# VectorE in GpSimd's place for four sums of the gate's weights

## The chip, the cores and the metric

One program on one core of a Trainium2 chip. The metric is the device time of one execution in microseconds (us). The engines are TensorE (PE: matmuls; PEld: its weight loads), VectorE (DVE), ScalarE (ACT), GpSimd (POOL) and SyncE (SP). GpSimd and SyncE here also issue the loads and stores.

## What is computed

One layer of a decoder trunk, 512 tokens, width 1024, float32: an RMS norm, one wide projection, a block-sparse attention branch and a gated recurrence branch, their merge, an output projection that is added to the residual, and last a gated embedding. The change lies in the last two lines:

```python
h = h + merged.astype(dt) @ w_out[i]
ple = (p[i] @ w_ple[i]).astype(f32) * jax.nn.sigmoid((h @ w_ple_gate[i]).astype(f32))
h = h + ple.astype(dt)
```

`h` is 512 x 1024 and `w_ple_gate` 1024 x 1024.

## The kernel before

Each float32 product is done as three matmuls of a reduced type. An operand is split in a high part (ScalarE copies it, rounding; names ending in `h`) and a low part (VectorE subtracts the high part from the operand; names ending in `l`), and high x high, low x high and high x low are summed. So every weight that arrives has to pass ScalarE and then VectorE before TensorE can use it.

The last stage, `h @ w_ple_gate`, is a 2 x 2 block product in seven half-size products instead of eight (Strassen's scheme in Winograd's form). `product(i, tt)` is one of two token tiles of product i: 12 matmuls of 128 x 512, four steps of the inner dimension k with three matmuls each. They run in the order 1, 5, 6, 7, 4, 3, 2, with the small products `pe` (the embedding, 6 matmuls a tile) between them. Results lie in the PSUM banks `ga`, `gb` and `gc`: products 6, 7 and 4 add up in the two `gb` banks, so before product 7 writes a bank, VectorE must have read it (`keepr = gb + keep`, L1348), and likewise `keepb` before product 4.

The operands of the seven products are sums and differences of blocks. Those of the tokens (`b..`, `bl`, `bt`, `bu`) come from `pairs_of_h`, out of the eight blocks `hf` of the residual (L1262); `b2l` of the fourth pair is the low part that product 1 needs for its last k step. Those of the weights come from `weights_of_g`, a generator that the code advances step by step: `a11`, `a22`, `a21` are blocks of the weight as loaded, of two tiles each, 128 x 1024. It makes

- `s1 = a21 + a22` for product 5 (L1143, tiles named `gs`), and in place `a11 = a11 - a21` for product 7 (L1145, tiles named `wf`): two instructions each, on GpSimd;
- `s1 = a22 - a11` for product 6 (L1152) and `s1 = a12 - s1` for product 3 (L1164), on VectorE;
- the high and low parts `w1h`, `w1l` to `w7h`, `w7l` in `halves_of`, on ScalarE and VectorE.

The weights of the stage are loaded by eight transfers of 512 KB on GpSimd's queue (L276), each as soon as its tile is free. Two of them stand between GpSimd's own sums, and the last two take the tiles of `a21`, which the differences L1145 read last.

The embedding's weights `w_p` (L1229 on SyncE's queue) pass one after the other through two slots of `pb`. A slot is filled again once VectorE has read it (`pwl`, L1231). ScalarE runs in order: behind the high parts `pwh` of these weights stand the high parts `w3h` and the sigmoids of the first output tiles. The two banks `pe` of the first embedding are free for the second when VectorE has multiplied them into the outputs (L1302).

TensorE's order is written out by hand. The order on the other engines is set by a list scheduler, from the dependencies, from priorities (`tc.high_priority`) and from edges that give an order only (`behind(inst, other)`); it decides from its own estimates, so a change to one instruction can move others.

## Time and profile before

| | |
|---|---|
| median of 3 runs | 449.94 us (449.64 to 450.37) |
| profiled execution | 449.9 us |
| its span, first to last instruction | 448.1 us |
| TensorE busy | 441.2 us, 98% |
| VectorE busy | 341.6 us, 76% |
| ScalarE busy | 287.5 us, 64% |
| GpSimd busy | 88.1 us, 20% |
| mean granted TensorE clock | 0.994 |

The profiled execution's time is 1.8 us above its span: what lies before the first and after the last instruction. A row of the timeline gives start, duration, engine, line, operation, output<-inputs, sizes, and in brackets how long the engine had been idle and what ended it. A row of VectorE or ScalarE covers the instruction's whole length, and the next one can begin a little before its end; the distance of two starts is what an instruction costs its engine when nothing holds it. Matmuls are pipelined: they show 0.39 us each and start every 0.227 us.

### The profile page before, as it was taken

The page shows a single profiled execution, that of the slowest core. Times are in us where ns is not written, and L with a number is a line of the kernel's source. Part 1 is how long each engine was busy: PE and PEld are TensorE (multiplying, and loading weights), DVE is VectorE, ACT ScalarE, POOL GpSimd, SP SyncE. Part 2 cuts the span into 40 slices and gives each one's busy share as a digit, 9 for nine tenths or more (in the row PEclk, how much of TensorE's full clock was granted, in tenths as well). Part 3 has the DMA queues.
Part 4 walks back from the last instruction along what each step waited for, and adds up shares of the span by engine and source line. Part 5 has one row for each costly group of instructions (what it writes and reads, how often), then busy time and mean ns, then how long its engine had stood idle before and what let it go on. Part 6 is the DMA issues. An engine that isn't in the chain of part 4 may idle for free.

```text
span 448.1 us, 7514 instructions
## 1 busy us (share of the span) xinstructions
PE 441.2 (98%) x2646; PEld 366.3 (82%) x2646; DVE 341.6 (76%) x662; ACT 287.5 (64%) x541; POOL 88.1 (20%) x147
## 2 busy tenths in 40 slices
PE   9999999999999999999999999999999999979996
PEld 8888888888888888888888888878888888868886
DVE  5869496777899797949888575565479779999852
ACT  5858584637779888967988697873234444355611
POOL 1000100000000432041403141501220103520242
PEclk9999999999999999999999999999999999989999
DMA  8803333357595463273423745455540666623222
GB/s 251 337 1 94 116 119 118 106 198 180 157 200 133 150 169 124 84 188 120 141 95 88 229 142 153 120 177 137 155 133 26 204 201 189 206 68 94 94 95 94
DMA packets 36709, 63.69 MB, mean 142 GB/s; under 512 B 7616, under 2 KB 19776, under 8 KB 36672
## 3 DMA queue, kind: packets, MB, share of 16 engines
q0 software_dynamic: 10848, 34.87, 25.2%
q1 hardware_dynamic: 25536, 28.27, 22.6%
q8 instruction: 21, 0.34, 0.3%
q14 instruction: 16, 0.13, 0.1%
q10 hardware_dynamic: 288, 0.07, 0.1%
HBM read 50.87 MB, written 7.08 MB: 129 GB/s over the span
## 4 chain that ended last, share of the span: by engine, by line
PE 95%; DVE 3%; issue 1%; ACT 0%; DVEq 0%
PE gb L305 10%; PE ga L305 10%; PE h L305 7%; PE bq L305 5%; PE ub L305 5%; PE bg L305 5%; PE ak L435 5%; PE ag L305 5%; PE bf L305 5%; PE ua L305 5%; PE aq L435 5%; PE av L435 5%; PE bi L435 5%; PE gb L1289 4%; PE gc L1289 2%; PE pe L1220 2%
## 5 line engine op out<-in xcount | busy, mean ns | idle before, releaser
L287 DVE TENSOR_TENSOR wl<-wf,wh 128x1024 fp32r<-128x1024 f32 (+1 forms) x70 | 76.6, 1095 | 32.9 <-ACT wh L286 31.5
L286 ACT ACTIVATE wh<-wf 128x1024 fp32r<-128x1024 f32 (+1 forms) x70 | 67.0, 957 | 49.3 <-PE ub L305 12.0
L276 POOL DMA_DIRECT2D wf<-in_w_tr_dram x30 | 16.2, 540 | 110.0 <-DVE wl L287 74.4
L924 POOL DMA_DIRECT2D pb<-pb x56 | 27.7, 501 | 36.5 <-DVE pb L913 16.1
L305 PE MATMUL ga<-xh,wh 128*128 128x512 f32 x64 | 25.2, 394 | 0.0
L305 PE MATMUL gb<-xh,wh 128*128 128x512 f32 x64 | 25.1, 393 | 0.0
L305 PE MATMUL ga<-xh,wl 128*128 128x512 f32 x64 | 24.9, 389 | 0.0
L305 PE MATMUL gb<-xl,wh 128*128 128x512 f32 x64 | 24.9, 389 | 0.0
L305 PE MATMUL ga<-xl,wh 128*128 128x512 f32 x64 | 24.9, 389 | 0.0
L305 PE MATMUL h<-mh,wh 128*128 128x512 f32 x64 | 24.9, 389 | 0.0
L305 PE MATMUL h<-ml,wh 128*128 128x512 f32 x64 | 24.9, 389 | 0.0
L305 PE MATMUL h<-mh,wl 128*128 128x512 f32 x64 | 24.9, 389 | 0.0
L305 PE MATMUL gb<-xh,wl 128*128 128x512 f32 x64 | 24.9, 389 | 0.0
L908 ACT ACTIVATE pb<-pb,ps 128x128 f32<-128x128 f32 (+3 forms) x32 | 17.6, 551 | 7.6 <-DVE ps L906 7.6
L276 POOL DMA_DIRECT2D wf<-in_w_tok_dram x8 | 4.4, 552 | 76.8 <-ACT avv L495 45.2
L1305 POOL TENSOR_TENSOR out<-out,pb 128x512 f32<-128x512 f32 (+1 forms) x8 | 10.3, 1300 | 38.9 <-DVE out L1302 38.8
L276 POOL DMA_DIRECT2D wf<-in_w_up_dram x16 | 8.7, 541 | 41.7 <-DVE wl L287 23.4
L910 ACT ACTIVATE pb<-pb,ps 128x128 f32<-128x128 f32 (+3 forms) x32 | 15.8, 550 | 0.1
L305 PEld LDWEIGHTS ga<-xh,wh 128*128 128x128 f32 x64 | 12.0, 188 | 2.8 <-issue 0.4
L305 PEld LDWEIGHTS gb<-xh,wh 128*128 128x128 f32 x64 | 12.0, 188 | 2.7 <-issue 0.2
L305 PEld LDWEIGHTS ga<-xh,wl 128*128 128x128 f32 x64 | 12.0, 188 | 2.6
L305 PEld LDWEIGHTS gb<-xh,wl 128*128 128x128 f32 x64 | 12.0, 188 | 2.5
(575 smaller groups left out, 1383.2 us busy)
## 6 DMA issues: line engine op xcount, KB each, us to landing
wf<-in_w_tr_dram POOLq DMA_DIRECT2D x30, 512.0 KB, 4.0
wf<-in_w_tok_dram POOLq DMA_DIRECT2D x8, 512.0 KB, 3.6
wf<-in_w_g_dram POOLq DMA_DIRECT2D x8, 512.0 KB, 4.2
wf<-in_w_up_dram POOLq DMA_DIRECT2D x16, 256.0 KB, 3.0
wf<-in_w_o_dram POOLq DMA_DIRECT2D x8, 512.0 KB, 4.4
wf<-in_w_tok_dram SPq DMA_DIRECT2D x6, 512.0 KB, 6.9
bias<-in_ed_dram SPq DMA_DIRECT2D x8, 256.0 KB, 5.1
xres<-in_xT_dram SPq DMA_DIRECT2D x8, 256.0 KB, 3.0
```

The lines of the kernel that those rows point to most:

```text
L276: (G if len(wraw) >= FAR else nc.sync).dma_start(raw, ap)
L286: rounds[i] = A.activation(hi, wraw[i], AF.Copy)
L287: low = V.tensor_tensor(lo, wraw[i], hi.bitcast(F32), op=OP.subtract)
L305: dense.append(PE.matmul(ps, a[:, k, :], b[k], start=(n == 0), stop=(n == tot - 1)))
L435: dense.append(PE.matmul(banks[t], a[:, s_], b[:, kk, :], start=(k == 0 and i == 0), stop=(k == KD - 1 and i == 2)))
L908: A.activation(p_, p_, AF.Exp, bias=st[:, 0:1], scale=-1.0, accum_out=st[:, 1:2])
L910: A.activation(p_, p_, AF.Copy, scale=st[:, 2:3])
L924: (G if both and b % 2 else nc.sync).dma_start(pt[32 * b:32 * b + 32, a], z[32 * a:32 * a + 32, b])
L1220: dense.append(PE.matmul(bk[:, c], a[:, ts_], b[:, c], start=(n == 0), stop=(n == 5)))
L1289: dense.append(PE.matmul(dst[i][tt][:, c], a[:, 128 * tt:128 * tt + 128], b[:, c], start=(k == 0 and m == 0 and i in (1, 6, 5)), stop=(k = ...
L1305: (adder or G).tensor_tensor(o3, o3, h_, op=OP.add)
```

## The change

The four instructions L1143 and L1145 go from GpSimd to VectorE. The low parts of product 7's third and fourth k step, made by the form of `halves_of` with its own tiles (`apart`), are written ahead of the other two in the code and get an edge that puts them behind the last low part made by the other form, which is product 6's (`w6l`).

```diff
             for k in range(2):
-                split(hs[k], ls[k], src[:, k])
+                A.activation(hs[k], src[:, k], AF.Copy)
+                low = V.tensor_tensor(ls[k], src[:, k], hs[k].bitcast(F32), op=OP.subtract)
+                if i == 7:
+                    behind(low, lows[-1])
             return list(zip(hs, ls))
...
-        V.tensor_tensor(l_, src, h_.bitcast(F32), op=OP.subtract)
+        lows.append(V.tensor_tensor(l_, src, h_.bitcast(F32), op=OP.subtract))
...
         for k in range(2):
-            G.tensor_tensor(s1[k], a21[k], a22[k], op=OP.add)
+            V.tensor_tensor(s1[k], a21[k], a22[k], op=OP.add)
         for k in range(2):
-            G.tensor_tensor(a11[k], a11[k], a21[k], op=OP.subtract)
+            V.tensor_tensor(a11[k], a11[k], a21[k], op=OP.subtract)
...
+        second = halves_of(7, 2, a11[1], "w7", "YB")
         halves_of(7, 0, a11[0], "w7")
-        wt[7].extend(halves_of(7, 2, a11[1], "w7", "YB"))
+        wt[7].extend(second)
```

Below, the order on VectorE at three places; TensorE's order is the same in both kernels. Line numbers behind the change are 1 to 4 higher (L1131 becomes L1134, L1143 L1146, L1145 L1148, L1152 L1155, L234 of these splits L1125). `pb` is scratch space of the token sums, `hf_4085` the last block but one of the residual, `w5l`, `w1l` low parts of the weights of products 5 and 1.

First, before product 1. Before:

```order
L1204 TENSOR_TENSOR pb<-hf_4034,pb 128x256
L234 TENSOR_TENSOR bl2l<-hf_4034,bl2h 128x512
L234 TENSOR_TENSOR bt2l<-pb,bt2h 128x512
L1210 TENSOR_TENSOR bu2l<-pb,bu2h 128x512
L234 TENSOR_TENSOR w5l_4117<-gs_4110,w5h_4115 128x512
L1262 TENSOR_TENSOR hf_4085<-h_4060,xres_4054 128x512
L1131 TENSOR_TENSOR w1l_4057<-wf_3942,w1h_4056 128x1024
L234 TENSOR_TENSOR w5l_4118<-gs_4110,w5h_4116 128x512
L1193 TENSOR_TENSOR pb<-hf_4085 128x256
L234 TENSOR_TENSOR b2l<-hf_4085,b2h 128x256
```

The same stretch on VectorE after the change:

```order
L1208 TENSOR_TENSOR pb<-hf_4034,pb 128x256
L1146 TENSOR_TENSOR gs_4110<-wf_4105,wf_3997 128x1024
L234 TENSOR_TENSOR bl2l<-hf_4034,bl2h 128x512
L234 TENSOR_TENSOR bt2l<-pb,bt2h 128x512
L1148 TENSOR_TENSOR wf_3881<-wf_3881,wf_4052 128x1024
L1214 TENSOR_TENSOR bu2l<-pb,bu2h 128x512
L1266 TENSOR_TENSOR hf_4085<-h_4060,xres_4054 128x512
L1125 TENSOR_TENSOR w5l_4117<-gs_4110,w5h_4115 128x512
L1134 TENSOR_TENSOR w1l_4057<-wf_3942,w1h_4056 128x1024
L1125 TENSOR_TENSOR w5l_4118<-gs_4110,w5h_4116 128x512
L1197 TENSOR_TENSOR pb<-hf_4085 128x256
L234 TENSOR_TENSOR b2l<-hf_4085,b2h 128x256
```

The second sum and the first difference now stand ahead of `b2l`. The first sum stands further up, between the previous `b2l` and `hf_4034`; the second difference stands right behind this `b2l`.

Second, the low parts for products 6 and 7 on VectorE. Before:

```order
L234 TENSOR_TENSOR bt3l<-pb,bt3h 128x256
L234 TENSOR_TENSOR w7l_4241<-wf_3942,w7h_4239 128x512
L1131 TENSOR_TENSOR w6l_4204<-gs_4109,w6h_4203 128x1024
L1131 TENSOR_TENSOR w6l_4208<-gs_4110,w6h_4207 128x1024
L1164 TENSOR_TENSOR gs_4109<-wf_4247,gs_4109 128x1024
```

The same stretch after the change:

```order
L234 TENSOR_TENSOR bt3l<-pb,bt3h 128x256
L1134 TENSOR_TENSOR w6l_4204<-gs_4109,w6h_4203 128x1024
L1134 TENSOR_TENSOR w6l_4208<-gs_4110,w6h_4207 128x1024
L1125 TENSOR_TENSOR w7l_4237<-wf_3942,w7h_4235 128x512
L1168 TENSOR_TENSOR gs_4109<-wf_4247,gs_4109 128x1024
```

The low part of product 7 went from ahead of the two `w6l` to behind them.

Third, on VectorE from the first `keepr` on. Before:

```order
L1348 TENSOR_TENSOR keepr_4167<-gb_4161,keep_4165 128x512
L1231 TENSOR_TENSOR pwl_4257<-pb,pwh_4256 128x512
L1131 TENSOR_TENSOR w4l_4288<-wf_3995,w4h_4287 128x1024
L1348 TENSOR_TENSOR keepr_4168<-gb_4162,keep_4166 128x512
L1131 TENSOR_TENSOR w4l_4292<-wf_3997,w4h_4291 128x1024
L1241 STREAM_TRANSPOSE restart<-hf_4148 128x4x4x32
```

The same stretch after the change:

```order
L1352 TENSOR_TENSOR keepr_4167<-gb_4161,keep_4165 128x512
L1134 TENSOR_TENSOR w4l_4288<-wf_3995,w4h_4287 128x1024
L1352 TENSOR_TENSOR keepr_4168<-gb_4162,keep_4166 128x512
L1134 TENSOR_TENSOR w4l_4292<-wf_3997,w4h_4291 128x1024
L1235 TENSOR_TENSOR pwl_4257<-pb,pwh_4256 128x512
L1245 STREAM_TRANSPOSE restart<-hf_4148 128x4x4x32
```

`pwl_4257`, which frees a slot of `pb` for the last of the embedding's weights, went behind three others. On ScalarE `pwh_4256` went behind the two `w4h` in the same way. On GpSimd only its loads are left in this stretch, in the same order.

## The prediction

> **What bounds the kernel now.** I read the head of the page and its chain first, then TensorE's waits, then the timelines of the engines around the one long wait.

> ```profile
> span 448.1 us, 7514 instructions
> PE 441.2 (98%) x2646; PEld 366.3 (82%) x2646; DVE 341.6 (76%) x662; ACT 287.5 (64%) x541; POOL 88.1 (20%) x147
> ...
> PE 95%; DVE 3%; issue 1%; ACT 0%; DVEq 0%
> ```

> TensorE is the bound: 98% of the span and 95% of the chain that ended last. Only what shortens TensorE's own row of work counts, so the next view is its waits.

> ```profile
> PE ga L1289 <- DVE b2l L234: 2.5, 1, 2.5
> ```

> There is one in all the kernel (beside the start): 2.5 us in product 1, for the low part `b2l`. TensorE's timeline there, and at two later points that I need:

> ```profile
> 392.76 0.39 PE L1289 MATMUL ga<-w1h,b2h 128*128 128x512 f32 x1
> 395.63 0.79 PE L1289 MATMUL ga<-w1h,b2l 128*128 128x512 f32 x1 [2.49 <-DVE b2l L234]
> ...
> 398.76 0.40 PE L1289 MATMUL ga<-w1l,b0h 128*128 128x512 f32 x1
> 399.00 0.39 PE L1289 MATMUL ga<-w1h,b2h 128*128 128x512 f32 x1
> ...
> 411.24 0.39 PE L1289 MATMUL gb<-w7h,bu0h 128*128 128x512 f32 x1
> ...
> 424.84 0.39 PE L1220 MATMUL pe<-pwh,ph 128*128 128x512 f32 x1
> ```

> From the first matmul of product 7 (411.24) to that of the second `pe` (424.84) stand 60 matmuls: 13.60 / 60 = 0.227 us each. So the matmul at 395.63 could have begun at 392.99: the stall cost 2.64 us. The eight matmuls from 395.63 to 399.00 took 3.37 us where 1.81 is normal: 1.56 more. The stretches show why (PEclk, the third figure from the right, is the granted clock):

> ```profile
> 395.63:399.00 3.37, 3.37 (x9) 2.67 (x9) 3.27 (x5) 2.09 (x4) 0.21 (x1) 0.54 0.49 156
> 399.00:411.24 12.24, 12.24 (x56) 10.13 (x54) 12.24 (x18) 7.59 (x13) 0.00 (x0) 1.00 0.17 45
> ```

> After the stall the clock was 0.54. Stall and slow spell make 4.20 us, the most that this place can give back. The second row also shows VectorE busy for all of 12.24 us: it is the next bound.

> Why `b2l` was late is seen in VectorE's timeline beside GpSimd's:

> ```profile
> 377.43 2.14 DVE L234 TENSOR_TENSOR b2l<-hf,b2h 128x256 fp32r<-128x256 f32 x1
> 380.04 0.69 DVE L1262 TENSOR_TENSOR hf<-h,xres 128x512 f32<-128x512 f32 x1 [0.47 <-PE h L305]
> ...
> 383.51 2.89 DVE L234 TENSOR_TENSOR bl2l<-hf,bl2h 128x512 fp32r<-128x512 f32 x1
> 386.32 2.89 DVE L234 TENSOR_TENSOR bt2l<-pb,bt2h 128x512 fp32r<-128x512 f32 x1
> 389.14 0.68 DVE L1210 TENSOR_TENSOR bu2l<-pb,bu2h 128x512 fp32r<-128x512 f32 x1
> 389.74 0.68 DVE L234 TENSOR_TENSOR w5l<-gs,w5h 128x512 fp32r<-128x512 f32 x1
> ...
> 392.68 2.57 DVE L1193 TENSOR_TENSOR pb<-hf 128x256 f32<-128x256 f32 x1
> 395.17 0.41 DVE L234 TENSOR_TENSOR b2l<-hf,b2h 128x256 fp32r<-128x256 f32 x1
> 395.73 0.42 DVE L234 TENSOR_TENSOR bt3l<-pb,bt3h 128x256 fp32r<-128x256 f32 x1
> 396.07 1.22 DVE L1152 TENSOR_TENSOR gs<-wf,wf 128x1024 f32<-128x1024 f32 x1
> 397.21 0.68 DVE L1262 TENSOR_TENSOR hf<-h,xres 128x512 f32<-128x512 f32 x1
> ```

> ```profile
> 376.89 2.40 POOL L1143 TENSOR_TENSOR gs<-wf,wf 128x1024 f32<-128x1024 f32 x1 [4.28 <-DMA wf<-in_w_g_dram]
> 379.24 0.57 POOL L276 DMA_DIRECT2D wf<-in_w_g_dram  x1
> 383.20 2.65 POOL L1143 TENSOR_TENSOR gs<-wf,wf 128x1024 f32<-128x1024 f32 x1 [3.40 <-DMA wf<-in_w_g_dram]
> 385.82 2.85 POOL L1145 TENSOR_TENSOR wf<-wf,wf 128x1024 f32<-128x1024 f32 x1
> ...
> 392.24 2.73 POOL L1145 TENSOR_TENSOR wf<-wf,wf 128x1024 f32<-128x1024 f32 x1 [2.71 <-DVE w1l L1131]
> ```

> Four VectorE rows are long, and each began inside one of GpSimd's four sums and ended 0.28 to 0.55 us after it (379.57 after 379.29; 386.40 after 385.85; 389.21 after 388.67; 395.25 after 394.97): they waited for it and then did their own work. The other rows of the same sizes take 0.42 and 0.68.

> **The change part by part.** *Removed from VectorE:* the waits. By starts, a 128x512 costs 0.60 (389.14 to 389.74), a 128x256 0.34 (395.73 to 396.07). `bl2l` and `bt2l` took 2.81 and 2.82, the `pb` row 2.49: 2.21 + 2.22 + 2.15 = 6.58 us won behind 380.04. The 1.80 of the row at 377.43 lies ahead of an `hf` that waited for TensorE anyway.

> *Added to VectorE:* four instructions of the kind at 396.07, same operation and size, 1.14 by starts. The first sum comes behind the row at 377.43, which then ends by 377.85, and is done before 379.1: `hf` still starts at 380.04, cost 0. The second sum and the first difference stand ahead of `b2l`, 2.28; the second difference behind it, 1.14.

> *Product 1.* `b2l` starts at 395.17 - 6.58 + 2.28 = 390.87 and ends by 391.3; TensorE wants it at 392.99. 1.7 us to spare, so stall and slow spell go: -4.20 for TensorE here.

> *Product 7.* TensorE now asks for it at 411.24 - 4.20 = 407.04, and it needs `keepr` read first:

> ```profile
> 404.51 1.05 ACT L1128 ACTIVATE w7h<-wf 128x1024 fp32r<-128x1024 f32 x1
> ...
> 410.15 0.68 DVE L1348 TENSOR_TENSOR keepr<-gb,keep 128x512 f32<-128x512 f32 x1
> 410.75 0.68 DVE L1231 TENSOR_TENSOR pwl<-pb,pwh 128x512 fp32r<-128x512 f32 x1
> ...
> 416.38 1.23 DVE L1131 TENSOR_TENSOR w3l<-gs,w3h 128x1024 fp32r<-128x1024 f32 x1 [0.89 <-ACT w3h L1128]
> ...
> 421.73 0.68 DVE L1302 TENSOR_TENSOR out<-out,pe 128x512 f32<-128x512 f32 x1
> ```

> VectorE has the same instructions ahead of `keepr` plus three: 410.15 - 6.58 + 3.42 = 406.99. One wait appears: with `w7l` behind the `w6l`, only two 128x256 rows lie between the subtraction L1155 and the `w6l` that needs ScalarE's copy of its result. The copy takes 1.05 (row at 404.51), so `w6l` can start 1.22 + 1.05 and two hand-overs of 0.05 (`b2l` ended at 395.58, TensorE began at 395.63) after the subtraction's start, 2.37, while VectorE is free after 1.14 + 0.34 + 0.34 = 1.82: 0.55 idle. That is the price of the new edge. A gap of 0.22 before (395.17 + 0.34 to 395.73) goes. So `keepr` starts at about 407.3, ends at 408.0, and TensorE stalls 1.0 us: of 4.20, 3.2 is left. What is late next is thus VectorE itself.

> *The second `pe`.* TensorE would ask for its bank 60 matmuls on, at 408.0 + 13.60 = 421.6. The bank comes free by the row at 421.73, which hangs on this chain: `pwl` at 410.75 frees the slot, the last `w_p` lands, ScalarE copies it, then `w3h`, then VectorE's `w3l` (idle 0.89 before it):

> ```profile
> 414.37 0.63 ACT L1230 ACTIVATE pwh<-pb 128x512 fp32r<-128x512 f32 x1 [0.79 <-DMA pb<-in_w_p_dram]
> 415.29 1.06 ACT L1128 ACTIVATE w3h<-gs 128x1024 fp32r<-128x1024 f32 x1 [0.29 <-PE gb L1289]
> ```

> This `pwl` now stands behind `w4l`, `keepr`, `w4l`: 407.3 + 0.60 + 1.14 + 0.60 + 1.14 = 410.8, no earlier than before. So `pwh` stays at 414.4; `w3h` no longer waits for TensorE and follows at 414.9, 0.4 earlier; the row at 421.73 moves to 421.3, ends at 422.0. TensorE stalls 0.4 and starts the second `pe` at 422.05 instead of 424.84: 2.8 us won.

> *The rest:* from there TensorE runs as before, with VectorE half idle.

> ```profile
> 424.84:443.88 19.04, 19.04 (x100) 16.47 (x98) 8.45 (x12) 3.96 (x7) 7.53 (x6) 1.00 0.29 101
> ```

> *GpSimd's queue:* the load at 379.24 no longer waits behind a sum; the last two wait for differences that end earlier than GpSimd's. Their cover is the 10 us until their first use; cost 0, gain 0.

> The sum against the profiled execution: 449.9 - 2.8 = 447.1, and its 449.9 is the median's 449.94.

> [...]

> **The rivals.**

> *Both new stalls fail to come:* `keepr` and the bank are in time, all 4.20 is kept: 445.7. For it: 1.0 and 0.4 are differences of long sums. Against: VectorE had no gap there, and before had only 0.4 in hand (`keepr` ended at 410.83, product 7 began at 411.24).

> *The 1.0 us stall drops the clock too:* 1.56 lost in product 7; the `pe` stall of 0.4 goes with it, so 447.1 + 1.1 = 448.2. No row shows a stall of that length; it is nearer to none than to 2.64.

> *A sum waits for its load on VectorE:* the first sum's load landed at 376.89 where it is wanted at 377.8, with 1.1 more before `hf` is late. It would have to land 4.8 us later to use up the 2.8: 449.9.

> *The long rows have another cause* and stay, transfers say: this ends slower. Then `keepr` starts 3.42 + 0.55 later, at 414.1, product 7 at 414.85 instead of 411.24: 453.5. It decides once less than 3.6 of the 6.58 goes. Against it: the stretch 360 to 370 has more DMA than 380 to 390 (0.70 against 0.60, second figure from the right) and no sum on GpSimd, and a row like `bl2l` took 0.68 there:

> ```profile
> 360.00:370.00 10.00, 10.00 (x46) 8.29 (x45) 7.62 (x13) 3.64 (x6) 1.06 (x2) 1.00 0.70 201
> 380.00:390.00 10.00, 10.00 (x45) 8.29 (x45) 9.93 (x10) 4.69 (x7) 6.04 (x3) 1.00 0.60 184
> ```

> ```profile
> 362.35 0.68 DVE L234 TENSOR_TENSOR bl0l<-hf,bl0h 128x512 fp32r<-128x512 f32 x1
> ```

> [...]

> **How the numbers follow.** Forecast 0.60 (446.6 to 447.6: a few tenths on each hand-over); full gain 0.13; clock drop 0.15; late load 0.06; long rows stay 0.06. About 0.2% (0.9 us) is what a measurement can tell from none. The first three are faster, 0.88; the late load is the same, 0.06; the last slower, 0.06. From the full gain, 445.6, to the clock drop with 0.4 for the hand-overs, 448.6, lie 0.88 of the chance.

> **What would show it.** Right: no VectorE row over 1.3 us between 376 and 396; no wait for `b2l`; PEclk 1.00 from 395 to 399; two TensorE waits, about 1.0 for `keepr` ahead of product 7 and 0.4 for `out` ahead of the second `pe`; 0.5 idle before `w6l`. Wrong: long rows that stay, a clock under 1.00 behind product 7's start, or a VectorE wait for a load of `w_g`.

## The result and the profile after

The changed kernel takes 447.25 us (median of 6 runs, 447.08 to 448.36) against 450.02 of the kernel before: a ratio of 0.9942, interval 0.9929 to 0.9955. Forecast were 447.1 and 445.6 to 448.6. The profiled execution took 447.09, its span 445.3, 2.8 us less than before. The page's head and chain, and TensorE's waits:

```profile
span 445.3 us, 7514 instructions
PE 439.7 (99%) x2646; PEld 364.1 (82%) x2646; DVE 338.1 (76%) x666; ACT 287.8 (65%) x541; POOL 76.3 (17%) x143
...
PE 97%; DMA 1%; ACT 0%; SPq 0%; DVE 0%; issue 0%; DVEq 0%
```

```profile
PE gb L1293 <- ACT w4h L1131: 0.9, 1, 0.9
```

The wait for `b2l` is gone. VectorE has left the chain (3% to 0%), and its busy time fell by 3.5 us although it does four instructions more: what it lost was waiting that the profile had counted as work. A wait of 0.9 us ahead of product 7 is new. (A further 0.3 in the attention branch stands in this profile and not in the second one of the same kernel; product 1 is no later for it, as its matmul at 392.71 stood at 392.76 before.) TensorE's timeline at the three places:

```profile
392.71 0.39 PE L1293 MATMUL ga<-w1h,b2h 128*128 128x512 f32 x1
392.94 0.39 PE L1293 MATMUL ga<-w1h,b2l 128*128 128x512 f32 x1
...
406.77 0.39 PE L1293 MATMUL gb<-w6l,bt3h 128*128 128x512 f32 x1
408.09 0.47 PE L1293 MATMUL gb<-w7h,bu0h 128*128 128x512 f32 x1 [0.94 <-ACT w4h L1131]
408.40 0.39 PE L1293 MATMUL gb<-w7h,bu0l 128*128 128x512 f32 x1
...
421.55 0.39 PE L1293 MATMUL gb<-w4l,bu3h 128*128 128x512 f32 x1
421.88 0.50 PE L1224 MATMUL pe<-pwh,ph 128*128 128x512 f32 x1
422.21 0.40 PE L1224 MATMUL pe<-pwh,pl 128*128 128x512 f32 x1
```

At `b2l` the matmuls follow each other every 0.23 us. Product 7 could have begun 0.227 after 406.77, at 407.00, and began at 408.09: 1.09 lost, and 0.08 more because the first matmul behind the stall took 0.31 (408.09 to 408.40) instead of 0.227. The second `pe` lost 0.10 and again 0.10 in its first matmul. Of the 4.20 that the place could give back, 1.37 went again: 2.83 is left, which is what the span shows. The clock stayed up in all of it (third figure from the right):

```profile
395.00:399.00 4.00, 4.00 (x19) 3.34 (x18) 3.65 (x7) 2.35 (x4) 0.00 (x0) 1.00 0.31 100
...
407.00:412.00 5.00, 4.07 (x18) 3.30 (x18) 5.00 (x8) 2.18 (x3) 0.00 (x0) 1.00 0.17 56
```

VectorE's rows that answer to those of before:

```profile
377.38 0.38 DVE L234 TENSOR_TENSOR b2l<-hf,b2h 128x256 fp32r<-128x256 f32 x1
377.69 1.22 DVE L1146 TENSOR_TENSOR gs<-wf,wf 128x1024 f32<-128x1024 f32 x1
379.99 0.69 DVE L1266 TENSOR_TENSOR hf<-h,xres 128x512 f32<-128x512 f32 x1 [1.09 <-PE h L305]
...
384.59 0.68 DVE L234 TENSOR_TENSOR bl2l<-hf,bl2h 128x512 fp32r<-128x512 f32 x1
385.20 0.69 DVE L234 TENSOR_TENSOR bt2l<-pb,bt2h 128x512 fp32r<-128x512 f32 x1
...
390.47 0.42 DVE L1197 TENSOR_TENSOR pb<-hf 128x256 f32<-128x256 f32 x1
390.80 0.43 DVE L234 TENSOR_TENSOR b2l<-hf,b2h 128x256 fp32r<-128x256 f32 x1
...
399.16 2.36 DVE L1134 TENSOR_TENSOR w6l<-gs,w6h 128x1024 fp32r<-128x1024 f32 x2 [0.52 <-ACT w6h L1131]
...
407.26 0.69 DVE L1352 TENSOR_TENSOR keepr<-gb,keep 128x512 f32<-128x512 f32 x1
...
410.72 0.69 DVE L1235 TENSOR_TENSOR pwl<-pb,pwh 128x512 fp32r<-128x512 f32 x1
...
421.13 0.68 DVE L1306 TENSOR_TENSOR out<-out,pe 128x512 f32<-128x512 f32 x1
```

The four long rows are short: 0.38, 0.68, 0.69, 0.42. The first sum fits in the idle time ahead of `hf`. Two lines belong to the price: 0.52 idle ahead of `w6l`, and `pwl` at 410.72, where it stood before the change.

### The profile page after: what moved, and what is told of

Same layout as the page of the kernel before. It is cut to its first block, busy times and chain, and to the rows that moved or that the text cites. A ratio compares the mean times of both kernels' runs of the same rounds, so it can differ in the third digit from the quotient of the medians.

```text
span 445.3 us, 7514 instructions
## 1 busy us (share of the span) xinstructions
PE 439.7 (99%) x2646; PEld 364.1 (82%) x2646; DVE 338.1 (76%) x666; ACT 287.8 (65%) x541; POOL 76.3 (17%) x143
## 4 chain that ended last, share of the span: by engine, by line
PE 97%; DMA 1%; ACT 0%; SPq 0%; DVE 0%; issue 0%; DVEq 0%
PE gb L305 10%; PE ga L305 10%; PE h L305 10%; PE av L435 5%; PE bq L305 5%; PE ub L305 5%; PE bg L305 5%; PE ak L435 5%; PE ag L305 5%; PE bf L305 5%; PE ua L305 5%; PE aq L435 5%; PE bi L435 4%; PE gb L1293 4%; PE ga L1293 2%; PE gc L1293 2%
## 5 line engine op out<-in xcount | busy, mean ns | idle before, releaser
L276 POOL DMA_DIRECT2D wf<-in_w_tr_dram x30 | 16.1, 538 | 109.7 <-DVE wl L287 81.6
L305 PE MATMUL ga<-xh,wh 128*128 128x512 f32 x64 | 25.2, 394 | 0.0
L305 PE MATMUL gb<-xh,wh 128*128 128x512 f32 x64 | 25.1, 393 | 0.0
L305 PE MATMUL ga<-xh,wl 128*128 128x512 f32 x64 | 24.9, 389 | 0.0
L305 PE MATMUL gb<-xl,wh 128*128 128x512 f32 x64 | 24.9, 389 | 0.0
L305 PE MATMUL ga<-xl,wh 128*128 128x512 f32 x64 | 24.9, 389 | 0.0
L305 PE MATMUL gb<-xh,wl 128*128 128x512 f32 x64 | 24.9, 389 | 0.0
L305 PE MATMUL h<-mh,wh 128*128 128x512 f32 x64 | 24.9, 389 | 0.0
L305 PE MATMUL h<-ml,wh 128*128 128x512 f32 x64 | 24.9, 389 | 0.0
L305 PE MATMUL h<-mh,wl 128*128 128x512 f32 x64 | 24.9, 389 | 0.0
L276 POOL DMA_DIRECT2D wf<-in_w_tok_dram x8 | 4.4, 550 | 76.8 <-ACT avv L495 45.1
L1309 POOL TENSOR_TENSOR out<-out,pb 128x512 f32<-128x512 f32 (+1 forms) x8 | 9.4, 1187 | 39.6 <-DVE out L1306 39.5
L276 POOL DMA_DIRECT2D wf<-in_w_up_dram x16 | 8.6, 540 | 41.8 <-DVE wl L287 28.1
L305 PEld LDWEIGHTS ga<-xh,wh 128*128 128x128 f32 x64 | 12.0, 188 | 2.8 <-issue 0.4
L305 PEld LDWEIGHTS gb<-xh,wh 128*128 128x128 f32 x64 | 12.0, 188 | 2.8 <-issue 0.2
L305 PEld LDWEIGHTS ga<-xh,wl 128*128 128x128 f32 x64 | 12.0, 188 | 2.5
L305 PEld LDWEIGHTS h<-ml,wh 128*128 128x128 f32 x64 | 12.0, 188 | 2.5
```

Source lines behind the costliest of these rows:

```text
L276: (G if len(wraw) >= FAR else nc.sync).dma_start(raw, ap)
L305: dense.append(PE.matmul(ps, a[:, k, :], b[k], start=(n == 0), stop=(n == tot - 1)))
L1309: (adder or G).tensor_tensor(o3, o3, h_, op=OP.add)
```

## The experiments

**Is the clash of GpSimd and VectorE the cause?** The changed kernel, with GpSimd reading the same tiles again, for nothing (`gd` is read by nobody):

```diff
             V.tensor_tensor(s1[k], a21[k], a22[k], op=OP.add)
+            for c in range(2):
+                G.tensor_tensor(gd, a21[k][:, c], a22[k][:, c], op=OP.add)
...
             V.tensor_tensor(a11[k], a11[k], a21[k], op=OP.subtract)
+            for c in range(2):
+                G.tensor_tensor(gd, a11[k][:, c], a22[k][:, c], op=OP.subtract)
```

> The changed kernel, and GpSimd does eight more additions of 128x512 out of the same weight tiles into a tile that nobody reads: two at each sum, two at each difference. Nothing on VectorE depends on them. My theory (a VectorE instruction with two inputs in SBUF and a GpSimd instruction that reads SBUF shut each other out for their whole length): VectorE rows of 0.4 to 1.2 us grow by up to 1.3 each where they meet one, b2l is late again, about 451.5 us (449.5 to 454). Rival (the rows were long for another cause, transfers for example): the rows keep their lengths, 447.2.

It took 454.59 us (ratio to the kernel before 1.0122, interval 1.0104 to 1.0139). Three rows of its GpSimd and six of its VectorE:

```profile
376.39 1.29 POOL L1149 TENSOR_TENSOR gd<-wf,wf 128x512 f32<-128x512 f32 x1 [4.13 <-DMA wf<-in_w_g_dram]
...
389.88 1.62 POOL L1153 TENSOR_TENSOR gd<-wf,wf 128x512 f32<-128x512 f32 x1 [5.63 <-DVE wf L1151]
...
392.04 1.28 POOL L1153 TENSOR_TENSOR gd<-wf,wf 128x512 f32<-128x512 f32 x1
```

```profile
376.45 0.70 DVE L1250 STREAM_TRANSPOSE sc<-hf 128x512 f32<-128x512 f32 x1
377.07 0.89 DVE L234 TENSOR_TENSOR b2l<-hf,b2h 128x256 fp32r<-128x256 f32 x1
...
389.66 0.68 DVE L1219 TENSOR_TENSOR bu2l<-pb,bu2h 128x512 fp32r<-128x512 f32 x1
390.26 0.68 DVE L1271 TENSOR_TENSOR hf<-h,xres 128x512 f32<-128x512 f32 x1
390.86 1.19 DVE L1125 TENSOR_TENSOR w5l<-gs,w5h 128x512 fp32r<-128x512 f32 x1
391.98 2.43 DVE L1134 TENSOR_TENSOR w1l<-wf,w1h 128x1024 fp32r<-128x1024 f32 x1
```

The long rows are back, though nothing on VectorE depends on what GpSimd does. `w1l` takes 2.43 instead of 1.22 and ends 1.09 after GpSimd's addition; the transpose, with one input, runs beside such an addition in its usual 0.70. `b2l` ends 0.28 after its addition: like the rows of before, a held row ends about its own length after GpSimd's. GpSimd is held too: its addition at 389.88, begun while `bu2l` ran, took 1.62 where the two others took 1.28 and 1.29. `hf`, which reads `h` from PSUM, ran in 0.68 beside that addition, and `w5l` behind it was held to 1.19. `w1l` even starts 0.06 ahead of the addition that holds it, so the starts do not tell which of two goes first. That shows the cause. The size I missed (451.5 was expected, 454 at most): four waits, not one, come of it, and the clock falls twice (to means of 0.61 and 0.63, shown further down).

```profile
PE gb L1298 <- DVE keepr L1357: 2.4, 1, 2.4
PE ga L1298 <- DVE w1l L1134: 2.1, 1, 2.1
...
PE gb L1298 <- DVE w6l L1134: 0.5, 1, 0.5
PE ga L1298 <- DVE b2l L234: 0.3, 1, 0.3
```

Then the same with fills in place of the additions; GpSimd's fills take 6.8 us in all, and only the 128x2 additions ahead of them read anything. The differences get the same:

```diff
+            G.tensor_tensor(gd[:, 0:2], a21[k][:, 0, 0:2], a22[k][:, 0, 0:2], op=OP.add)
+            for c in range(3):
+                G.memset(gd, 0.0)
```

> The changed kernel, with twelve fills of 128x512 on GpSimd (three at each sum and each difference, into a tile that nobody reads, each three behind an addition of 128x2 that only fixes their moment): GpSimd writes SBUF for some 6 us in all but reads none. My theory (VectorE and GpSimd shut each other out over reads): the rows of VectorE keep their lengths but for the moments of the small additions, 447.4 us. Rival (any work of GpSimd on SBUF holds VectorE up): rows of VectorE grow by 0.5 and more where a fill meets them, and the time goes to 450 or more.

447.42 us (0.9946, 0.9934 to 0.9957); the changed kernel on the same chip had 446.82. A fill and the rows of VectorE beside it:

```profile
387.80 1.72 POOL L1155 MEMSET gd<- 128x512 f32 x3
```

```profile
387.75 0.68 DVE L1125 TENSOR_TENSOR w5l<-gs,w5h 128x512 fp32r<-128x512 f32 x1
388.35 1.22 DVE L1134 TENSOR_TENSOR w1l<-wf,w1h 128x1024 fp32r<-128x1024 f32 x1
```

**What does the edge do?** The sums left on GpSimd, all else as in the changed kernel:

```diff
-            V.tensor_tensor(s1[k], a21[k], a22[k], op=OP.add)
+            G.tensor_tensor(s1[k], a21[k], a22[k], op=OP.add)
...
-            V.tensor_tensor(a11[k], a11[k], a21[k], op=OP.subtract)
+            G.tensor_tensor(a11[k], a11[k], a21[k], op=OP.subtract)
```

> The edge and the changed order of the code alone; the four sums stay on GpSimd. My theory: the wait for b2l and the slow clock stay as before (2.5 us and about 1.5), w6l waits about 0.5 for ScalarE and the stall before product 7 is 0.2 at most: 450.0 us, no difference to before. Rival (the edge brings a good part of the gain): 448.5 or less.

449.91 us, 1.001 of the time before (1.000 to 1.002): nothing. The `b2l` wait is 2.5 us as before, and product 7 has a wait of 0.2. The other way round, the sums moved and the edge left out:

```diff
-                if i == 7:
-                    behind(low, lows[-1])
```

> The four sums on VectorE as in the changed kernel, without the edge that puts the low parts of product 7 behind those of product 6. My theory (VectorE's row of work sets product 7 and, over the slot that pwl frees, the second pe; the edge costs about 0.5 us of VectorE idle): no idle before w6l, keepr 0.5 earlier, stall before product 7 about 0.4 instead of 0.9, the pwl of the last embedding weight one 128x1024 earlier and so no second stall: 446.1 us. Rival (the edge is what makes the change pay, since without it low parts of product 7 delay product 6): 447.5 or more, with a wait for w6l in TensorE's waits.

445.50 us, 0.9915 (0.9901 to 0.9930), faster than the changed kernel. As that comparison was made on another occasion, both ran again side by side:

> The changed kernel once more, unchanged, so that it stands beside the other three on the same chip. Both theories: 0.994 of the time before.

> The kernel without the edge once more, beside the changed one on the same chip. My theory (the edge costs VectorE 0.5 us ahead of product 7): 0.9 to 1.4 us under the changed kernel. Rival (the difference of the two in separate comparisons was that of the chips): within 0.4 us of it.

446.82 (0.9937, 0.9921 to 0.9952) with the edge and 445.83 (0.9914, 0.9902 to 0.9927) without. The two intervals overlap a little, so the 1.0 us between the medians leans on the traces, of which each version has two. With the edge both show 0.94 of waiting ahead of product 7, and the first 0.52 idle ahead of `w6l`. Without it the wait is 0.32 in one and 0.33 in the other, and in the first `w6l` follows without idle time. The first trace without the edge:

```profile
399.77 2.36 DVE L1132 TENSOR_TENSOR w6l<-gs,w6h 128x1024 fp32r<-128x1024 f32 x2
...
406.65 0.68 DVE L1350 TENSOR_TENSOR keepr<-gb,keep 128x512 f32<-128x512 f32 x1
...
408.98 0.69 DVE L1233 TENSOR_TENSOR pwl<-pb,pwh 128x512 fp32r<-128x512 f32 x1
...
418.09 0.68 DVE L1304 TENSOR_TENSOR out<-out,pe 128x512 f32<-128x512 f32 x1
```

```profile
407.48 0.47 PE L1291 MATMUL gb<-w7h,bu0h 128*128 128x512 f32 x1 [0.32 <-DVE keepr L1350]
```

`keepr` comes 0.61 earlier. `pwl` comes 1.74 earlier, and the multiplication that frees the bank 3.04 earlier: on ScalarE `w3h` (411.65) now stands ahead of the high part of the last of the embedding's weights (412.62); with the edge it stood behind it (414.72 after 414.18). The order of ScalarE changed here too, so the earlier slot is not shown to be the only reason. The second `pe` starts without a gap, at 421.20.

**Is `keepr` what product 7 waits for?** In the changed kernel the profile names ScalarE's `w4h`. Without the edge, and with two instructions of VectorE that are not urgent put behind the first `keepr` (`reads[0]`):

```diff
-            V.tensor_tensor(s1[k], wraw[r + 6 + k], s1[k], op=OP.subtract)
+            behind(V.tensor_tensor(s1[k], wraw[r + 6 + k], s1[k], op=OP.subtract), reads[0])
```

> Without the edge, and the two subtractions for product 3 (128x1024 each, needed only some 6 us later) are put behind the first keepr on VectorE. My theory (what stalls TensorE before product 7 is VectorE coming late to keepr): keepr starts as soon as product 6 is done, about 404.4, TensorE has no wait left behind the start, another 0.3 to 0.5 us under the kernel without the edge, about 445.1 us if that is 445.5. Rival (the wait is for ScalarE's w4h, which the profile of the changed kernel names): a wait of 0.3 or more stays before product 7 and the time does not move.

TensorE has no wait left behind its start, and product 7 begins 0.23 after the last matmul of product 6:

```profile
407.20 0.39 PE L1291 MATMUL gb<-w6l,bt3h 128*128 128x512 f32 x1
407.43 0.39 PE L1291 MATMUL gb<-w7h,bu0h 128*128 128x512 f32 x1
```

```profile
407.53 1.04 ACT L1129 ACTIVATE w4h<-wf 128x1024 fp32r<-128x1024 f32 x1
```

It begins while the second `w4h` has not yet started. So product 7 does not need `w4h`; the profile of the changed kernel names it because it ended last there (at 408.02, `keepr` at 407.95). The other traces agree: in those of the changed kernel, of the edge alone, of the sums moved without the edge, of the one difference moved and of the eight additions, all with a stall there, product 7 begins 0.14 to 0.15 us after the end of `keepr`, whichever engine is named. In the time the last step does not show, and here the rival's forecast, no change, came true: 445.92 us, 0.9906 (0.9893 to 0.9920), against 445.83 and 0.9914 on the same chip. The runs of one kernel differ by 0.8 to 1.6 us, more than the 0.3 to 0.5 us in question. This is the fastest version by its ratio but not by its median, and no run separates it from the one without the edge.

**Does only `b2l` count, and when does the clock fall?** One of the four instructions moved, the one that held the row ahead of `b2l`:

```diff
-            V.tensor_tensor(s1[k], a21[k], a22[k], op=OP.add)
+            G.tensor_tensor(s1[k], a21[k], a22[k], op=OP.add)
...
-            V.tensor_tensor(a11[k], a11[k], a21[k], op=OP.subtract)
+            (G, V)[k].tensor_tensor(a11[k], a11[k], a21[k], op=OP.subtract)
```

> Only the last of the four (the second difference) is done by VectorE, with the edge; the other three stay on GpSimd. My theory: the two 2.9 us rows bl2l and bt2l stay, the long row just ahead of b2l goes; b2l is late by about 0.4 instead of 2.6, the clock stays up there; but VectorE is still behind, keepr starts at about 409.5 and TensorE stalls 2.7 before product 7. If a stall of that length drops the clock there as it did at b2l: 450.5 us; if not: 448.9. Rival (b2l is the only place where VectorE's lateness counts): 446.3.

448.77 us, 0.9988 (0.9979 to 0.9996): the case without a clock drop, and far from the rival's 446.3. The row ahead of `b2l` is short (0.41), while the two long rows left are `bt2l` and `bu2l`, 2.88 and 2.89, where I had expected `bl2l` and `bt2l`. `b2l` is late by only 0.3, but VectorE is still behind:

```profile
PE gb L1293 <- DVE keepr L1352: 1.7, 1, 1.7
...
PE gc L1293 <- DVE w5l L1134: 0.4, 1, 0.4
PE ga L1293 <- DVE b2l L234: 0.3, 1, 0.3
```

The stall was 1.7 and not 2.7, since a wait for `w5l` that I had not counted, and the one for `b2l`, had held TensorE up already; `keepr` began at 409.34 where I had put it at about 409.5, and product 7 at 410.17. So the run does not say what a stall of 2.7 would do. After the one of 1.7 the clock was 1.00:

```profile
410.17:413.00 2.83, 2.83 (x12) 2.33 (x13) 2.83 (x4) 1.64 (x3) 0.00 (x0) 1.00 0.72 187
```

Two places of the kernel with the eight additions, behind the stalls of 2.36 and 2.12, in this order:

```profile
414.40:417.60 3.20, 3.20 (x9) 2.59 (x10) 3.20 (x4) 0.63 (x1) 0.00 (x0) 0.63 0.35 87
394.46:395.73 1.27, 0.99 (x2) 0.30 (x3) 1.27 (x4) 0.36 (x1) 0.00 (x0) 0.61 0.01 3
```

There the mean is 0.6. Behind the longer stall the fall came late, with the fourth matmul; from there to the end of the slow spell the starts of full speed (0.23 apart) became starts 0.37 and then 0.42 to 0.43 apart:

```profile
414.40 0.47 PE L1298 MATMUL gb<-w7h,bu0h 128*128 128x512 f32 x1 [2.36 <-DVE keepr L1357]
...
415.17 0.57 PE L1298 MATMUL gb<-w7h,bu1h 128*128 128x512 f32 x1
415.54 0.63 PE L1298 MATMUL gb<-w7h,bu1l 128*128 128x512 f32 x1
...
418.82 0.39 PE L1298 MATMUL gb<-w7h,bu0h 128*128 128x512 f32 x1
```

By the mean clock, the fall did not come in every execution of the kernel before. Beside these runs the kernel before was measured again, 23 times on one chip. In 10 executions its mean clock was 0.994 to 0.996, as in the profiled one, whose only stretch of matmuls below 1 is the one behind `b2l` (0.54); in 13 it was 0.998 to 1.000. The medians are 449.9 and 449.1 us. On the other chip it was 6 to 5, with 449.9 and 449.7. No trace of an execution without the drop was kept; that it had the same wait is assumed, since the program is the same. So of the 2.8 us won, up to some 0.8 (an estimate from these medians) hangs on a drop that comes in about half of the executions.

## Why the prediction was right

By its own steps, what was forecast and what the trace shows:

| step | forecast | trace |
|---|---|---|
| long rows of VectorE gone | none over 1.3 | none over 1.23 |
| first sum | cost 0 | `hf` at 379.99, 1.09 idle before it |
| `b2l` starts | 390.87 | 390.80 |
| idle ahead of `w6l` | 0.55 | 0.52 |
| `keepr` starts | 407.3 | 407.26 |
| stall ahead of product 7 | 1.0, clock stays up | 1.09, clock 1.00 |
| late `pwl` | 410.8 | 410.72 |
| second `pe` starts | 422.05 | 421.88 |
| gain | 2.8 | 2.8 |

The stall ahead of the second `pe` was mis-sized: 0.4 forecast, 0.10 measured. Against the forecast, product 7 began 0.09 later (it begins 0.14 after `keepr` ends, where the forecast had it begin at that end) and its first matmul took 0.08 more, which moved TensorE's asking to 421.78, and the bank came free 0.2 earlier. The first matmuls behind the two stalls took 0.08 and 0.10 more than 0.227, which I had not counted. These errors nearly cancel, so that the total agrees to a tenth is in part luck; so is that the profiled execution, from which the 4.20 was taken, was one with the clock drop. The mechanism, the long rows and the order of the later stalls, is as forecast.

Of the rivals, the other cause for the long rows fell with the two runs that gave GpSimd idle work, and the late load with the trace: no VectorE instruction waits for a load of `w_g`. The full gain did not come in the changed kernel; in its trace the ordering of VectorE took a third of it back, and without the edge and with the two late subtractions the stalls go. The clock drop after a stall of about 1 us did not happen: behind the wait of 0.94 the clock was 1.00. That it would stay up, as the forecast had it, was my estimate; no row of before showed a stall of that length.

The forecast named the change as one thing. The runs show that it was two, which pull against each other: moving the sums gives the whole gain, and the edge alone gives nothing and takes about 1 us (by the medians side by side) when the sums have moved.

## What to carry to other kernels

An instruction whose row is several times longer than others of its size (here 2.89 against 0.68) can be waiting, not working: look for what runs on the neighbour engine in just that stretch before counting it as load. Moving work on to the busier engine can then free it, as here, where VectorE's busy time fell by 3.5 us with four instructions more. When a stall of the bounding engine goes, the engine that feeds it must keep up with the new pace: work out for each later hand-over how much earlier the feeding engine itself comes and how much it had in hand, since no more than the two together can be kept. Here `keepr` came 2.89 us earlier (410.15 to 407.26) and had ended 0.41 before product 7 began, of which the hand-over needs 0.14; product 7 began 3.15 earlier, not 4.20.

## What the runs showed of the hardware

- In the profiled executions the matmul clock fell after waits of 2.12 and 2.36 us (the eight additions) and of 2.49 (the kernel before), to means of 0.61, 0.63 and 0.54 over the stretches shown, and stayed at 1.00 after 0.32 (without the edge), 0.94 (the changed kernel) and 1.74 (one difference moved). By the mean clock it fell in 16 of 34 executions of the kernel before. Where it fell, the slow matmuls took 1.56 us more than at full speed (eight of them, in the kernel before) and 1.70 (twelve, from 414.40 to 418.82).
- Beside GpSimd's fills of 0.5 to 0.6 us each VectorE's subtractions took 0.68 (`w5l`, 128x512) and 1.22 (`w1l`, 128x1024), as without them. GpSimd's additions held them: the held rows shown ended 0.28 (128x256), 0.54 to 0.55 (128x512) and 1.09 us (128x1024) after the addition, where such rows cost 0.34, 0.60 and 1.14 by their starts when nothing held them.
- Where product 7 waited, the profile's name for the wait was wrong (`w4h` for `keepr`), and an experiment with the order told it: product 7 began at 407.43, the second `w4h` at 407.53.
